# Two-layer hybrid backbone: the low parts of the weights by a negation on ScalarE and an accumulating DMA, with weight sub-blocks as halves of k

## The chip, the cores and the metric

The kernel runs on one NeuronCore of a Trainium2 chip. The metric is the device time of one launch in microseconds (us). Its engines are named as in the profile: PE (TensorE, the matmuls; PEld is its weight load), ACT (ScalarE), DVE (VectorE), POOL (GpSimd), and SP (SyncE, which here only issues DMAs). Each works through its own list of instructions in order.

## What is computed

One sample of 512 latent tokens (a grid of 64 columns) with a context of 256 tokens, 1024 features, goes through two layers. The first mixes by neighbourhood attention (8 heads of 64) beside four bidirectional gated recurrent heads (HGRN2), the second by a short gated convolution; each is followed by a gated feed-forward network (FFN) with 2816 inner features. Shift, scale and gate vectors come from the conditioning vector. All inputs are float32.

```python
def short_conv_mixer(h, w_in, conv_w, conv_b, w_out):
    gate_b, gate_c, u = jnp.split(h @ w_in, 3, axis=-1)
    return (gate_b * dwconv3(gate_c * u, conv_w, conv_b)) @ w_out

def conv_ffn(h, w_up, conv_w, conv_b, w_down):
    a, val = jnp.split(h @ w_up, 2, axis=-1)
    return (jax.nn.gelu(dwconv3(a, conv_w, conv_b), approximate=False) * val) @ w_down
...
for layer in range(DEPTH):
    mod = silu_c @ ada_w[layer] + ada_b[layer]
    shift_m, scale_m, gate_m, shift_f, scale_f, gate_f = jnp.split(mod, 6, axis=-1)
    ...
    h = modulate(rms_norm(x, norm_mix_w[layer]), shift_m, scale_m)
    if is_even:
        y, y_ctx = even_mixer(h, h_ctx, ev_w_in[j], ev_w_out[j], ...)
    else:
        y = short_conv_mixer(h, od_w_in[j], od_conv_w[j], od_conv_b[j], od_w_out[j])
    x = x + gate_m[:, None, :] * y
    h = modulate(rms_norm(x, norm_ffn_w[layer]), shift_f, scale_f)
    x = x + gate_f[:, None, :] * conv_ffn(h, ffn_w_up[layer], ...)
return rms_norm(x, final_norm_w)
```

## The kernel before

**Matmuls in two parts.** Every large product is done in float32r with operands split exactly into a high and a low part. `mm3` (L245) issues three matmuls for one tile of 128 rows of the contraction: high weight by high activation, high weight by low activation, low weight by high activation (L246, L247, L248). The third is the only one that reads the low part of the weights. Activations are feature-major, tiles of 128 features by 512 tokens.

**The weight stream.** All large weights are read once, in the order of a list called `plan` (L157 and on). An entry of the plan is a chunk of 256 columns by up to 1024 rows (1 MB), which SP loads into one of two raw buffers `wraw` of 128 x 2048 (`_load`, L59). A chunk has two sub-blocks. For the dense layers (`cols` L158, `rows_cols` L164) these are halves of the columns: all eight tiles of k, 128 columns each, so that a sub-block is all the weight of one output tile. For the recurrent and attention heads (`two`) the chunk is put together from two column groups. The first two chunks and the last projection (`wide`) have sub-blocks of four k tiles by 256 columns.

**The split.** `Weights.conv` (L65) makes a sub-block's parts: ACT copies the raw weights into `whi` (L84), which rounds them to float32r, and DVE subtracts the copy from the raw weights into `wlo` (L85). `whi` and `wlo` have three buffers each, 128 x 1024. `get(ahead)` (L93) returns the next sub-block and emits the splits up to `ahead` sub-blocks further, so in the dense layers a split stands in the program one sub-block ahead of its use, and its copy waits until PE has read the sub-block three places earlier. A raw buffer is free for the next load when both its sub-blocks are split. Sub-blocks are numbered 0 to 201 in the order of their use below.

**The order of the program.** After a start (norms, first adaptive vectors) come the values of the recurrent heads (sub-blocks 0 to 3, PSUM tiles `pvl`, `pvc`), then the mixer: a list of background tasks (`Weave`) puts the recurrent heads' scans (DVE, with small products `kb`, `qb`, `qi` on POOL), the attention and the adaptive vectors of the later stages (`Ada`, loads `ar` of 256 KB on SP's queue, L443) between the projections' matmuls. The first two output tiles of the output projection (`w_first`, L910, PSUM `pbo00` and `pbo01`) are built up as the attention heads finish, in the order of k = 4, 0, 5, 1, 2, then 6, 7, then 3. From there on the dense rest: `project_back` (L986) multiplies back to 1024 features, two tiles at a time, adds to the stream and collects the norm; its last two tiles go by halves of the tokens (256 each) so that the norm overlaps, with some spare buffers for sub-blocks split ahead (L1001). `quad` (L1054) does the first four tiles of the next stage by halves of the tokens, `pair` (L1046) two tiles of the following ones. `ffn_up` (L1087) takes pairs alternately from the two halves of the up projection (PSUM `ppa`, `ppv`), with the convolution (`conv3`: one ACTIVATE on ACT, L1072, two instructions on DVE), a GELU on ACT and the product. Accumulators have six PSUM buffers in the dense rest. The last projection (`down`, L1194) is token-major.

Of the kernel before, what the change touches and what calls it, by code (L numbers as in the profile page):

```python
# [9 lines left out]
F32 = mybir.dt.float32  # L10
# [28 lines left out]
class Weights:  # L39
    """Streams weight chunks and splits each sub-block exactly into two float32r parts."""  # L40
# [24 lines left out]
    def conv(self):  # L65
        """Split the next sub-block."""
# [18 lines left out]
        self.pin(self.nc.vector.tensor_tensor(lv, rv, hv.bitcast(F32), ALU.subtract))  # L85
# [48 lines left out]
def backbone(ctx: ExitStack, tc: tile.TileContext, a, out, dump=None):  # L134
# [13 lines left out]
    # ---------------------------------------------------------------- pools  # L148
# [6 lines left out]
    # ---------------------------------------------------------------- weight plan  # L155
    ktiled = lambda w: w.rearrange("(k p) c -> p k c", p=P)

    def cols(w, c0):  # L158
        return [([ktiled(w)[:, :, c0 : c0 + 256]], [(0, 0, w.shape[0] // P, j, j + P) for j in (0, P)])]
# [4 lines left out]
    def rows_cols(w, k0, k1, c0):  # L164
        return ([ktiled(w)[:, k0:k1, c0 : c0 + 256]], [(0, 0, k1 - k0, j, j + P) for j in (0, P)])
# [13 lines left out]
    plan += cols(w_in, 3840)  # L179
# [21 lines left out]
    # ---------------------------------------------------------------- constants  # L201
# [18 lines left out]
    # ================================================================ start  # L220
# [13 lines left out]
    def gate(h, src):  # L234
        """Output gate of a recurrent head with its norm weight."""
# [14 lines left out]
    def rms(srcs, n, nm, pool, aux):  # L250
        """Reciprocal root mean square over the features."""
# [35 lines left out]
    with ExitStack() as st:  # L287
# [37 lines left out]
        # (1 + bias) * norm weight  # L325
# [3 lines left out]
        # adaptive shift and scale of latents and context, one feature tile at a time;  # L329
        # row blocks of the weights go to the four column groups of the array  # L330
# [31 lines left out]
        # sum of squares: odd tiles straight on the tensor engine  # L362
# [40 lines left out]
        # lower bounds of the forget gates  # L403
# [27 lines left out]
    # ---------------------------------------------------------------- remaining adaptive vectors  # L431
# [554 lines left out]
    def project_back(nm, src, groups, gate, norm, start=0):  # L986
# [5 lines left out]
        for n, (mp_, gi) in enumerate(steps):  # L992
# [5 lines left out]
            if n == len(steps) - 1:  # L998
                break
# [282 lines left out]
```

## Time and profile before

| | |
|---|---|
| median of 3 runs | 1355.35 us (1355.1 to 1356.38) |
| span of the profiled execution, first to last instruction | 1353.2 us; its device time is not given apart from the runs |
| instructions | 19127 |
| DMA | 172.21 MB, mean 127 GB/s |
| weights: loads of `wraw` | 8 to 44 of each matrix, most of 1024 KB |
| adaptive weights: loads of `ar` | 160 of 256 KB |

The page gives the busy time of each engine and its share of the span, then groups of instructions by source line: the busy time, the mean of one in ns, and how long the engine stood idle ahead of them and for what. A busy PE is not PE at its peak; idle time of an engine that is not the limit costs nothing. In the timeline a row is the start, the length, the engine, the line and the operation with its tiles, and, in brackets, the idle time ahead of it and what ended it.

### The profile page before, as it was taken

How to read it: one execution, taken by the hardware profiler on the slowest of the kernel's cores; microseconds unless marked ns; L12 is line 12 of the kernel's file. 1: busy time of each engine (PE TensorE's matmuls, PEld its weight loads, DVE VectorE, ACT ScalarE, POOL GpSimd, SP SyncE). 2: the span in 40 equal slices, each digit the busy share in tenths (PEclk: the TensorE clock that was granted, in tenths of full speed). 3: DMA queues.
4: the chain of work that ended last, by engine and by line, in shares of the span. 5: the costliest groups of instructions: out<-in, count | busy, mean ns of one | idle time of the engine just before them, and what ended most of it. 6: DMA issues, size and time to landing. Idle time of an engine off the chain costs nothing. (4 is left out here: it accounts for less than half of the span.)

```text
span 1353.2 us, 19127 instructions
## 1 busy us (share of the span) xinstructions
PE 1330.6 (98%) x7736; PEld 1134.4 (84%) x7736; DVE 819.5 (61%) x1354; ACT 527.8 (39%) x815; POOL 84.4 (6%) x87
## 2 busy tenths in 40 slices
PE   7999999999999999999999999999999999999997
PEld 4797888888879888888888898888998888889997
DVE  4668788687777645555566675557766544442333
ACT  4533444555555433333322253223443333333223
POOL 2204322321000000000000000000000000000000
PEclk9999999999999999999999999999999999999999
DMA  9942112466454233333366633444423222332231
GB/s 295 267 127 65 32 32 78 117 159 178 146 168 143 90 117 128 124 118 117 109 192 196 211 126 125 149 143 152 147 86 124 94 94 95 102 101 84 86 110 63
DMA packets 170824, 172.21 MB, mean 127 GB/s; under 512 B 14320, under 2 KB 144752, under 8 KB 170736
## 3 DMA queue, kind: packets, MB, share of 16 engines
q1 hardware_dynamic: 168736, 166.15, 39.3%
q10 hardware_dynamic: 2000, 4.85, 1.4%
q8 instruction: 60, 0.98, 0.3%
q14 instruction: 28, 0.23, 0.1%
HBM read 165.21 MB, written 2.10 MB: 124 GB/s over the span
## 5 line engine op out<-in xcount | busy, mean ns | idle before, releaser
L84 ACT CAST whi<-wraw 128x1024 fp32r<-128x1024 f32 (+1 forms) x202 | 207.8, 1031 | 471.1 <-PE ppv L247 93.5
L85 DVE TENSOR_TENSOR wlo<-wraw,whi 128x1024 fp32r<-128x1024 f32 (+1 forms) x202 | 242.7, 1203 | 218.9 <-ACT whi L84 217.6
L247 PE MATMUL ppa<-hf,whi 128*128 128x512 f32 (+1 forms) x448 | 161.6, 361 | 0.0
L246 PE MATMUL ppa<-hf,whi 128*128 128x512 f32 (+1 forms) x448 | 161.2, 360 | 0.0
L248 PE MATMUL ppa<-hf,wlo 128*128 128x512 f32 (+1 forms) x448 | 160.2, 358 | 0.0
L247 PE MATMUL ppv<-hf,whi 128*128 128x512 f32 x320 | 126.1, 394 | 0.0
L246 PE MATMUL ppv<-hf,whi 128*128 128x512 f32 x320 | 125.8, 393 | 0.0
L248 PE MATMUL ppv<-hf,wlo 128*128 128x512 f32 x320 | 124.3, 388 | 0.0
L462 DVE SCALAR_TENSOR_TENSOR aa<-ar,sil,aa 128x512 f32<-128x512 f32 x140 | 105.1, 751 | 15.2 <-DMA ar<-in_ada_w_dram 13.7
L1198 PE MATMUL pd<-whi,g 128*128 128x256 f32 x352 | 98.1, 279 | 0.0
L1200 PE MATMUL pd<-wlo,g 128*128 128x256 f32 x352 | 98.0, 278 | 0.0
L1199 PE MATMUL pd<-whi,g 128*128 128x256 f32 x352 | 97.7, 278 | 0.0
L246 PEld LDWEIGHTS ppa<-hf,whi 128*128 128x128 f32 x448 | 84.1, 188 | 13.9
L248 PEld LDWEIGHTS ppa<-hf,wlo 128*128 128x128 f32 x448 | 84.1, 188 | 13.2
L247 PEld LDWEIGHTS ppa<-hf,whi 128*128 128x128 f32 x448 | 84.2, 188 | 12.2
L1109 DVE TENSOR_TENSOR ppv<-ppv,cv 128x512 f32<-128x512 f32 x40 | 28.0, 699 | 86.1 <-PE ppv L248 86.1
L246 PE MATMUL pbd<-g,whi 128*128 128x512 f32 (+1 forms) x192 | 72.3, 377 | 0.0
L247 PE MATMUL pbd<-g,whi 128*128 128x512 f32 (+1 forms) x192 | 72.0, 375 | 0.0
L248 PE MATMUL pbd<-g,wlo 128*128 128x512 f32 (+1 forms) x192 | 71.7, 373 | 0.0
L246 PEld LDWEIGHTS ppv<-hf,whi 128*128 128x128 f32 x320 | 60.1, 188 | 13.8
L248 PEld LDWEIGHTS ppv<-hf,wlo 128*128 128x128 f32 x320 | 60.1, 188 | 13.4
L247 PEld LDWEIGHTS ppv<-hf,whi 128*128 128x128 f32 x320 | 60.2, 188 | 11.9
(340 smaller groups left out, 2885.3 us busy)
## 6 DMA issues: line engine op xcount, KB each, us to landing
wraw<-in_ffn_w_up_dram SPq DMA_DIRECT2D x44, 1024.0 KB, 5.0
ar<-in_ada_w_dram SPq DMA_DIRECT2D x160, 256.0 KB, 2.8
wraw<-in_ffn_w_down_dram SPq DMA_DIRECT2D x16, 1024.0 KB, 5.1
wraw<-in_od_w_in_dram SPq DMA_DIRECT2D x12, 1024.0 KB, 5.2
wraw<-in_ev_w_in_dram SPq DMA_DIRECT2D x20, 512.0 KB, 5.3
araw<-in_ada_w_dram SPq DMA_DIRECT2D x16, 512.0 KB, 6.1
wraw<-in_ffn_w_down_dram SPq DMA_DIRECT2D x8, 768.0 KB, 4.9
wraw<-in_ev_w_out_dram SPq DMA_DIRECT2D x4, 1024.0 KB, 6.8
```

What stands on the lines that cost most here:

```text
L84: self.nc.scalar.copy(hv, rv)
L85: self.pin(self.nc.vector.tensor_tensor(lv, rv, hv.bitcast(F32), ALU.subtract))
L246: TE.matmul(o, wh, mh, start=start, stop=False, skip_group_check=True)
L247: TE.matmul(o, wh, ml, start=False, stop=False, skip_group_check=True)
L248: TE.matmul(o, wl, mh, start=False, stop=stop, skip_group_check=True)
L462: pin(V.scalar_tensor_tensor(self.acc[:], raw[:], sil[:, r, 0:1], self.acc[:], ALU.mult, ALU.add))
L1109: V.tensor_tensor(ov[i][:], ov[i][:], t[i][:], ALU.mult)
L1198: TE.matmul(o[i][:, 0:256], gh[:, ts], w[0][:, k - k0], start=k == 0, stop=False)
L1199: TE.matmul(o[i][:, 0:256], gl[:, ts], w[0][:, k - k0], start=False, stop=False)
L1200: TE.matmul(o[i][:, 0:256], gh[:, ts], w[1][:, k - k0], start=False, stop=k == FT - 1)
```

## The change

Three things change.

1. **The low part.** ACT writes the negated weights, rounded to float32r into `wlo` (`scalar.mul` by -1.0, L85 of the changed kernel), and an accumulating DMA on POOL's queue adds the raw float32 weights onto it (L86), which leaves raw minus high, as before. DVE has no part in it. There are 202 such DMAs, most of 512 KB from SBUF to SBUF, 128 rows of 4 KB.
2. **The sub-blocks.** In `cols` and `rows_cols` a sub-block is now half of the k tiles with all 256 columns, so that its rows are contiguous in the raw buffer. The function `blk` picks a tile's weights for one k from the list of sub-blocks.
3. **The order of use.** `pair` fetches the first half of k, does both output tiles with it, then the second half; `project_back` does the same, and its splits ahead (`ws.ahead(4)`, with the spare buffers) come after the first half. `w_first` and `quad` keep their order of k and tiles and take the weights by `blk`. The last chunk of the input projection (L179) becomes two column groups.

Comments are gone in the changed file and lines have moved by two to sixteen.

```diff
     def conv(self):
...
         self.nc.scalar.copy(hv, rv)
-        self.pin(self.nc.vector.tensor_tensor(lv, rv, hv.bitcast(F32), ALU.subtract))
+        self.nc.scalar.mul(lv, rv, -1.0)
+        self.nc.gpsimd.dma_start(lv.bitcast(F32), rv, accum_op=ALU.add)
...
     def cols(w, c0):
-        return [([ktiled(w)[:, :, c0 : c0 + 256]], [(0, 0, w.shape[0] // P, j, j + P) for j in (0, P)])]
+        return [rows_cols(w, 0, w.shape[0] // P, c0)]
...
     def rows_cols(w, k0, k1, c0):
-        return ([ktiled(w)[:, k0:k1, c0 : c0 + 256]], [(0, 0, k1 - k0, j, j + P) for j in (0, P)])
+        h = (k1 - k0 + 1) // 2
+        return ([ktiled(w)[:, k0:k1, c0 : c0 + 256]], [(0, 0, h, 0, 256), (0, h, k1 - k0, 0, 256)])
...
-    plan += cols(w_in, 3840)
+    plan.append(two(w_in, 3840, 3968))
...
+    def blk(w, i, k):
+        n = w[0][0].shape[1]
+        return [v[:, k % n, i * P : (i + 1) * P] for v in w[k // n]]
...
-                mm3(o_first[i][:], w_first[i][0][:, k], w_first[i][1][:, k], hh, hl, k == 4, k == 3)
+                wh, wl = blk(w_first, i, k)
+                mm3(o_first[i][:], wh, wl, hh, hl, k == 4, k == 3)
...
     def project_back(nm, src, groups, gate, norm, start=0):
...
-            w = [ws.get(), ws.get()]
+            w = [ws.get()]
             first, lastg = gi == 0, gi == len(groups) - 1
             if n == len(steps) - 1:
+                w.append(ws.get())
                 break
+            if n < len(steps) - 2 or len(groups) > 1:
+                units(4)
+            mid = k0 + (k1 - k0 + 1) // 2
+            for i in range(2):
+                mms(o, w, i, src, k0, k0, mid, slice(0, T), first, False)
+            w.append(ws.get())
             if n == len(steps) - 2:
                 ws.spare = [(gq, f"q{2 * i}", f"q{2 * i + 1}") for i in range(3)]
                 ws.ahead(4)
-            if n < len(steps) - 2 or len(groups) > 1:
-                units(4)
             for i in range(2):
-                mms(o[i], w[i], src, k0, k0, k1, slice(0, T), first, lastg)
+                mms(o, w, i, src, k0, mid, k1, slice(0, T), False, lastg)
...
     def pair(nm, src):
-        w = [ws.get(), ws.get()]
         o = [acc_t(f"pp{nm}{i}") for i in range(2)]
-        for i in range(2):
-            mms(o[i], w[i], src, 0, 0, KT, slice(0, T), True, True)
+        w = []
+        for k in (0, 4):
+            w.append(ws.get())
+            for i in range(2):
+                mms(o, w, i, src, 0, k, k + 4, slice(0, T), k == 0, k == 4)
         return o
```

**At the start, on ACT.** The rows from the last tile of the first norm on, before: `whi0` and `whi1` are the high parts of sub-blocks 0 and 1, `sqac` is the context's norm (its logarithm reads PE's sum `prc`), `sgq` are gates, `hc` the context's norm tiles.

```order
L270 ACTIVATE h0_7_92<-xs7_117,mod_77,amul_81 128x512
L84 CAST whi0_581<-wraw0_577 128x1024
L264 ACTIVATE sqac_521<-prc_556,epsc_73 128x256
L84 CAST whi1_595<-wraw0_577 128x1024
L265 ACTIVATE sqac_521<-sqac_521 128x256
L418 ACT_TABLE_LOAD
L418 ACTIVATE sgq0_615<-pq0_201 128x512
L270 ACTIVATE hc0_93<-ct0_199,mod_77,amul_81 128x256 x3
```

The same place of the change, where `wlo0` and `wlo1` written by L85 are the negations:

```order
L272 ACTIVATE h0_7_92<-xs7_117,mod_77,amul_81 128x512
L84 CAST whi0_581<-wraw0_577 128x1024
L266 ACTIVATE sqac_521<-prc_556,epsc_73 128x256
L85 ACTIVATE wlo0_582<-wraw0_577 128x1024
L267 ACTIVATE sqac_521<-sqac_521 128x256
L84 CAST whi1_596<-wraw0_577 128x1024
L272 ACTIVATE hc0_93<-ct0_199,mod_77,amul_81 128x256 x2
L85 ACTIVATE wlo1_597<-wraw0_577 128x1024
```

The negation of sub-block 0 stands where the copy of sub-block 1 stood, behind the logarithm, and that copy has moved behind the exponential.

**At the first output columns, on ACT and PE.** ACT of the change from the copy of sub-block 27 on; `gg` is a sigmoid gate, `vn`, `pe`, `pT` and `mnh` are attention's values, exponentials, transposed exponentials and outputs.

```order
L84 CAST whi27_3932<-wraw13_3582 128x1024
L239 ACT_TABLE_LOAD
L239 ACTIVATE gg2_3788<-pg2_3722 128x512
L805 COPY vn3_3764<-pvt3_3765 128x512
L810 COPY vn3_3764<-pvu3_3774 128x256
L830 ACT_TABLE_LOAD
L830 ACTIVATE pe300_3818,sm300_3815<-ps300_3810,sm300_3815 128x512
L244 CAST mgh2_3803<-gg2_3788 128x512
L830 ACTIVATE pe301_3836,sm301_3833<-ps301_3828,sm301_3833 128x512
L855 CAST mnh2_3851<-pno2_3341 128x4x8x16
L840 COPY pT300_3860<-pt300_3855 128x512
L85 ACTIVATE wlo27_3933<-wraw13_3582 128x1024
```

The copy's place and the rows behind it are those of before; the negation is the last row, behind all of them. PE's first matmuls of these columns, before:

```order
L246 MATMUL pbo00_3914<-mgh0_2687,whi26_3766 128x512
L247 MATMUL pbo00_3914<-mgl0_2688,whi26_3766 128x512
L248 MATMUL pbo00_3914<-mgh0_2687,wlo26_3767 128x512
L246 MATMUL pbo00_3914<-mnh0_2974,whi26_3766 128x512
L247 MATMUL pbo00_3914<-mnl0_2975,whi26_3766 128x512
```

The change:

```order
L248 MATMUL pbo00_3944<-mgh0_2705,whi27_3932 128x512
L249 MATMUL pbo00_3944<-mgl0_2706,whi27_3932 128x512
L248 MATMUL pbo01_3945<-mgh0_2705,whi27_3932 128x512
L250 MATMUL pbo00_3944<-mgh0_2705,wlo27_3933 128x512
L248 MATMUL pbo00_3944<-mnh0_2995,whi26_3793 128x512
```

The first matmuls used to read sub-block 26 (all k of the first tile); now they read 27 (k from 4 on, both tiles). PE's last matmuls of the same columns, before:

```order
L246 MATMUL pbo00_3914<-mnh3_4076,whi26_3766 128x512
L247 MATMUL pbo00_3914<-mnl3_4077,whi26_3766 128x512
L248 MATMUL pbo00_3914<-mnh3_4076,wlo26_3767 128x512
L246 MATMUL pbo01_3915<-mnh3_4076,whi27_3904 128x512
L247 MATMUL pbo01_3915<-mnl3_4077,whi27_3904 128x512
L248 MATMUL pbo01_3915<-mnh3_4076,wlo27_3905 128x512
```

The change:

```order
L248 MATMUL pbo00_3944<-mnh3_4106,whi26_3793 128x512
L249 MATMUL pbo00_3944<-mnl3_4107,whi26_3793 128x512
L250 MATMUL pbo00_3944<-mnh3_4106,wlo26_3794 128x512
L248 MATMUL pbo01_3945<-mnh3_4106,whi26_3793 128x512
L249 MATMUL pbo01_3945<-mnl3_4107,whi26_3793 128x512
L250 MATMUL pbo01_3945<-mnh3_4106,wlo26_3794 128x512
```

Sub-block 26 is now read up to the very last row, three matmuls longer; sub-block 29 takes its buffer.

**In the mixer, on POOL.** The change's rows around the first recurrent head's products, where `fg`, `fc` and `tb` are small fills and `wlo7` and `wlo8` the low parts of sub-blocks 7 and 8:

```order
L86 DMA wlo6_1101<-wraw3_914 128x1024
L573 MEMSET fg01_1238 128x2
L86 DMA wlo7_1217<-wraw3_914 128x1024
L560 MEMSET fc01_1232 128x2
L591 MEMSET tb10_1430 128x2
L610 TENSOR_TENSOR kb00_1196<-kn00_1124,cv00_1153 128x256
L610 TENSOR_TENSOR qb00_1198<-qn00_1123,cv00_1153 128x256
L604 TENSOR_TENSOR qi00_1200<-qn00_1123,cv00_1153 128x512
L573 MEMSET fg10_1359 128x2
L86 DMA wlo8_1338<-wraw4_1097 128x1024
```

Before, the same list held the fills and the products alone.

More of the change, by code (lines that the diff above doesn't have):

```diff
@@ L930, in backbone, with mms @@
     HALF = (slice(0, TC), slice(TC, T))
-    def mms(o, w, src, base, k0, k1, c, first, last):
-        wh, wl = w
+    def mms(o, w, i, src, base, k0, k1, c, first, last):
         for k in range(k0, k1):
             hh, hl = src[k]
-            mm3(o[:, c], wh[:, k - base], wl[:, k - base], hh[:, c], hl[:, c], first and k == base, last and k == k1 - 1)
+            wh, wl = blk(w, i, k - base)
+            mm3(o[i][:, c], wh, wl, hh[:, c], hl[:, c], first and k == base, last and k == k1 - 1)
     class Norm:
@@ L1013, in project_back @@
         ws.ahead(4)
-        mms(o[0], w[0], src, k0, k0, k1, A, first, True)
+        mms(o, w, 0, src, k0, k0, k1, A, first, True)
         norm.back(o[0], 6, A, gate)
@@ L1061, in quad @@
                     hh, hl = src[k]
-                    mm3(o[i][:, c], w[i][0][:, k], w[i][1][:, k], hh[:, c], hl[:, c], k == 0 and c.start == 0,
+                    wh, wl = blk(w[i // 2 * 2 : i // 2 * 2 + 2], i % 2, k)
+                    mm3(o[i][:, c], wh, wl, hh[:, c], hl[:, c], k == 0 and c.start == 0,
                         k == KT - 1)
```

8 lines of the change are left out of this document (4 added, 4 removed).

## The prediction, made before the changed kernel was run

> **What bounds the kernel now.** I read the page first, then PE's waits, then short stretches of the timeline around the weight splits.
>
> ```profile
> span 1353.2 us, 19127 instructions
> PE 1330.6 (98%) x7736; PEld 1134.4 (84%) x7736; DVE 819.5 (61%) x1354; ACT 527.8 (39%) x815; POOL 84.4 (6%) x87
> PEclk9999999999999999999999999999999999999999
> L84 ACT CAST whi<-wraw 128x1024 fp32r<-128x1024 f32 (+1 forms) x202 | 207.8, 1031 | 471.1 <-PE ppv L247 93.5
> L85 DVE TENSOR_TENSOR wlo<-wraw,whi 128x1024 fp32r<-128x1024 f32 (+1 forms) x202 | 242.7, 1203 | 218.9 <-ACT whi L84 217.6
> ```
>
> TensorE is busy for 1330.6 of 1353.2 us, with its granted clock in the top tenth in every slice. 22.6 us are not busy, so no edit that leaves the matmuls as they are can win more than that. The 202 copies at 1031 ns on ACT and 202 subtractions at 1203 ns on DVE take 450 us of two engines that have room. What counts is whether a low part is there when its first matmul is due.
>
> ```profile
> PE pkc L584 <- DVE sc L567: 2.1, 2, 1.5
> PE pt L836 <- DVE pe L830: 1.3, 4, 0.5
> 102.00:136.00 34.00, 31.87 (x208) 27.15 (x206) 30.95 (x45) 11.39 (x21) 14.61 (x13) 1.00 0.21 60
> 476.00:510.00 34.00, 34.00 (x150) 27.92 (x149) 16.92 (x20) 12.49 (x17) 0.00 (x0) 1.00 0.33 109
> ```
>
> The first two rows are PE's longest waits for DVE (total, times, longest), 3.4 us together; the others give the busy time of PE, PEld, DVE, ACT and POOL in a stretch, then clock, DMA share and GB/s. In the mixer (102 to 136) DVE is busy for 30.95 of 34 us and PE lacks 2.1. In an FFN (476 to 510) PE has no gap: 34.00 us for 150 matmuls, 0.227 each, so one sub-block of 24 takes 5.4 us.
>
> **How late a low part may be.** One sub-block of the FFN, from its copy to its first low matmul:
>
> ```profile
> 502.52 1.05 ACT L84 CAST whi<-wraw 128x1024 fp32r<-128x1024 f32 x1 [3.95 <-PE ppa L247]
> 503.47 0.77 ACT L1072 ACTIVATE cv<-ppa,vec 128x512 f32<-128x512 f32 x1
> 503.60 1.23 DVE L85 TENSOR_TENSOR wlo<-wraw,whi 128x1024 fp32r<-128x1024 f32 x1 [3.01 <-ACT whi L84]
> 513.99 0.39 PE L248 MATMUL ppv<-hf,wlo 128*128 128x512 f32 x1
> ```
>
> The copy starts when PE gives a buffer of the ring of three back, at 502.52; the low part is read first at 513.99, 11.5 us later, and is ready at 504.83. In the new form ACT takes 1.05 for the copy and as much for the negation, which moves the same elements (by the 0.77 of a 512-element ACTIVATE it could be 1.5). The accumulating transfer, from POOL's issue to its landing, may then take 11.5 - 2.1 = 9.4 us before PE notices, or 8.6 where such an ACTIVATE stands ahead of the negation. I call its length L.
>
> **What L is.** The trace has no accumulating transfer and none from POOL's queue. The nearest rows:
>
> ```profile
> wraw<-in_ffn_w_up_dram SPq DMA_DIRECT2D x44, 1024.0 KB, 5.0
> ar<-in_ada_w_dram SPq DMA_DIRECT2D x160, 256.0 KB, 2.8
> QS<-QS ACTq DMA_DIRECT2D x8, 256.0 KB, 2.9
> KS<-kl ACTq DMA_DIRECT2D x8, 192.0 KB, 3.9
> q1 hardware_dynamic: 168736, 166.15, 39.3%
> ```
>
> A line through 256 KB in 2.8 and 1024 KB in 5.0 gives 3.5 us for 512 KB. An accumulation must also read what it adds to; as 1 MB of traffic it takes 5.0. For POOL's own issue, which no row shows, I allow 1.0. **I take L = 6.0**, nearest to the 1 MB row. The ends are 3.3 (2.9 and an issue of 0.4, the adding free) and 11.5 (two passes of 5.0 one after the other, issue 1.5).
>
> The Trainium skill, in "Collectives: The Full Stack", section "The bandwidth ceiling: the fold count and why AG ≠ RS ≠ AR", says that an adding transfer runs at half of a copy's rate because it reads two sources, not because adding costs. With the fixed 2.0 us and 436 GB/s of "DMA: Bandwidth & Descriptors", section "Anatomy of one DMA", that makes an estimate of 4.4 us; the same fit gives 4.4 for the 1 MB load that took 5.0 here, so this trace is slower than the page, and by the page the sum would be about +3 us.
>
> **Where L = 6 shows.** The steady stages hide it with 2.6 us or more. The short places, in order:
>
> ```profile
> 59.34 1.03 ACT L84 CAST whi<-wraw 128x1024 fp32r<-128x1024 f32 x1
> 61.16 0.47 ACT L264 ACTIVATE sqac<-prc,epsc 128x256 f32<-128x256 f32 x1 [0.79 <-PE prc L263]
> 61.53 1.04 ACT L84 CAST whi<-wraw 128x1024 fp32r<-128x1024 f32 x1
> 65.41 0.28 PE L537 MATMUL pvl<-wlo,h 128*128 128x256 f32 x1
> ```
>
> *Start, sub-block 0.* The new order puts ACT's logarithm (L264 here), which waits for PE, between copy and negation. The negation takes the slot of the second copy: 61.53 + 1.04 = 62.57, + 6.0 = 68.6, against 65.41: **+3.2 us**. PE runs its queue in order and can put nothing in its place.
>
> ```profile
> 370.50 0.59 ACT L838 COPY pT<-pt 128x512 f32<-128x512 f32 x1
> 375.64 0.40 PE L248 MATMUL pbo<-mgh,wlo 128*128 128x512 f32 x1
> ```
>
> *First output columns, sub-block 27.* The order of ACT shows its negation behind the whole group of sigmoid, exponentials and copies, after the first pT copy, which ends at 371.1; 372.1 + 6.0 = 378.1. As the half with k from 4 to 7 it is now wanted first, one matmul after the place at 375.64: 375.9. **+2.3 us** (the ACT and PE rows under the change).
>
> ```profile
> 395.45 0.39 PE L248 MATMUL pbo<-mnh,wlo 128*128 128x512 f32 x1
> 395.65 2.00 ACT L84 CAST whi<-wraw 128x1024 fp32r<-128x1024 f32 x2 [1.69 <-PE pbo L247]
> 396.13 0.39 PE L248 MATMUL pbo<-mnh,wlo 128*128 128x512 f32 x1
> 402.31 0.39 PE L248 MATMUL pbo<-mnh,wlo 128*128 128x512 f32 x1
> 395.00:405.00 10.00, 10.00 (x45) 8.24 (x44) 7.63 (x9) 4.22 (x5) 0.00 (x0) 1.00 1.03 342
> 398.07 0.38 SPq L59 DMA_DIRECT2D wraw<-in_ev_w_out_dram  x1
> ```
>
> *Output projection, sub-block 29* takes 26's buffer. 26 now serves both tiles of the first columns, so its last matmuls are those at 396.13 and no longer those at 395.45 (the PE rows under the change): its copy moves by 0.68 from 395.65 to 396.33. Copy and negation end at 398.4, + 6.0 = 404.4, against 402.31: +2.1. It falls in ten microseconds whose DMA share is 1.03 already; I add 1.5, less than half of a 1 MB load. **+3.6.**
>
> ```profile
> 406.28 1.05 ACT L84 CAST whi<-wraw 128x1024 fp32r<-128x1024 f32 x1 [3.40 <-DMA wraw<-in_ev_w_out_dram]
> 409.95 0.63 ACT L958 ACTIVATE sqf<-xT 128x512 f32<-128x512 f32 x1 [2.62 <-DVE xT L953]
> 413.13 0.38 SPq L59 DMA_DIRECT2D wraw<-in_ffn_w_up_dram  x1
> 418.56 0.28 PE L248 MATMUL pbo<-mnh,wlo 128*128 128x256 f32 x1
> 431.11 0.28 PE L248 MATMUL ppa<-hf,wlo 128*128 128x256 f32 x1
> ```
>
> *Sub-blocks 32 and 36.* A raw buffer is now given back by the transfer. The load for 32 and 33, issued at 398.07 when 29's subtraction ended, is issued at 405.9 (404.4 + 1.5) and takes 5.0 to 8.2 (398.07 to 406.28); with 6 it lands at 411.9. Two copies, a square of 0.63 and two negations make 416.7, + 6.0 = 422.7, against 418.56 + 3.6: **+0.5**. The load for 36, at 413.13 now, follows at 422.7 and lands 5.0 later; copy, square, negation (2.7) and 6.0 make 436.4, against 431.11 + 4.1: **+1.2**.
>
> ```profile
> 673.28 1.05 ACT L84 CAST whi<-wraw 128x1024 fp32r<-128x1024 f32 x1 [3.95 <-PE ppv L247]
> 682.41 0.40 PE L248 MATMUL pbd<-g,wlo 128*128 128x512 f32 x1
> 680.00:782.00 102.00, 102.00 (x450) 83.41 (x449) 63.53 (x98) 25.18 (x28) 0.00 (x0) 1.00 0.65 204
> ```
>
> *First FFN's projection back.* Its shortest sub-blocks have 682.41 - 673.28 = 9.1 us, so L may be 7.0; they come at four places, and loads hold 0.65 of the DMA engines: a quarter of a microsecond each, **+1.0**.
>
> **What else moves.** ACT gains 202 x 1.03 = 208 us and stands at 736 of 1353, DVE loses 243; neither is near its end. In the dense stages a load follows the second split of its buffer and is wanted three copies later, 3 x 5.5 - 2.3 = 14.2 us; less 5.0 for the load and 5.8 because the buffer comes back later (1.05 + 6.0 against 1.23), 3.4 are left: hidden. On POOL the transfers stand in order among the mixer's products (the POOL rows under the change); both wait for an ACT that is busy 11.39 of 34 us, and the low parts there have time, as this mixer sub-block's copy and first low matmul show, 27.4 us apart:
>
> ```profile
> 153.09 1.03 ACT L84 CAST whi<-wraw 128x1024 fp32r<-128x1024 f32 x1
> 180.52 0.39 PE L248 MATMUL pf<-h,wlo 128*128 128x512 f32 x1
> ```
>
> In the pairs of the dense stages both tiles now end within 2.7 us instead of 5.4; six accumulators cover that. DVE's relief returns part of the 3.4 us: **-1.0** (between 0 and -3.4).
>
> **Sum:** 3.2 + 2.3 + 3.6 + 0.5 + 1.2 + 1.0 - 1.0 = +10.8 us. The median of the runs lies 2.2 us above this execution's span, and I move both alike: 1355.35 + 10.8 = **1366.2 us**.
>
> **Rivals.**
> *All covered.* With L at 4.2 or less the start costs at most 1.4, sub-blocks 27 and 29 0.5 and 0.3, with up to 1.5 more for the crowd there; less 1.0 that is at most +2.7: 1355 to 1358. For it: the 2.9 of the SBUF-to-SBUF row. Against: 192 KB took 3.9 on the same queue.
> *DVE's relief wins, faster.* In the mixer the subtraction stands in DVE's order behind a copy that waits for PE (217.6 us of DVE's idle time ended with such a copy), and the scans that feed PE stand behind it. Without it up to 3.4 us return; at L = 3.3 the stalls add to under 1: 1355.35 - 3.4 + 0.6 = 1352.6 or less. It decides if L is under 3.8 and these waits hang on the subtraction; but a scan that is long itself stays.
> *Transfers collide, L = 7 to 9.* q1's 39.3% for 166.15 MB is 3.2 us of all engines per MB. The 102 us of the projection back hold 450 matmuls, 19 sub-blocks, 10 MB: a share of 0.65 + 0.31, or 1.27 if an accumulation counts double, and over 1.0 it stretches. L = 8 adds 2 to sub-blocks 0, 27, 29 and 36 and 1.5 to the four places: 1380. L = 9 adds 3 to the one, 2.5 to the others and 0.4 to each of 40 FFN pairs: 1404. The Trainium skill knows a second route there, in "SBUF — State Buffer", section "Who interferes with whom": while DVE runs certain copies, the descriptors of a transfer issued by GpSimd wait. No row here shows it.
> *The adding itself is slow.* At L = 11.5 a buffer's turn is 2.1 + 11.5 + 5.4 = 19.0, a third of which is 6.3 per sub-block instead of 5.5; 160 dense sub-blocks make +130 us, 1485. It decides from 9.4 on.
>
> **Chances.** Forecast (L 5 to 7) 0.48; all covered 0.18; relief 0.09; collisions 0.17; slow adding 0.08. 0.2% is 2.7 us, about what a measurement of this kernel can tell from no change. Faster 0.09, same 0.18, slower 0.73. The forecast's own range is 1361 (L = 5) to 1371 (L = 7). The range from 1353 to 1400 leaves out the slow adding, most of the relief and the end of the collisions, 0.17.
>
> **What would show it.** The rows of the accumulating transfers give L: 5 to 7 right, under 4.2 or over 9 wrong. PE's waits for wlo should be 3 us at the first pvl, 2 at the first pbo of sub-block 27, 3 to 4 near 402, and none in the FFN pairs; if the pairs show waits, the sum is wrong by a multiple. If the waits at L584 are gone, the relief was sized too low. DVE should fall to about 577 us and ACT rise to 736.

## The result and the profile after

| | before | after |
|---|---|---|
| median, us | 1355.37 (4 runs, 1355.1 to 1356.38) | 1460.38 (4 runs, 1448.28 to 1462.9) |
| ratio | | 1.0755, 95% interval 1.0714 to 1.0795 |
| span of the profiled execution, us | 1353.2 | 1461.1 |

The changed kernel is 105 us slower, ten times the forecast's +10.8 and outside its range. The page of the changed kernel, the busy rows, TensorE's clock, the DMA engines' busy tenths and POOL's queue (packets, MB, share of the engines' time):

```profile
span 1461.1 us, 19760 instructions
PE 1368.3 (94%) x7736; PEld 1156.8 (79%) x7736; DVE 609.3 (42%) x1152; ACT 714.0 (49%) x1017; POOL 242.9 (17%) x289
PEclk9999999899999999999999989999999999999999
DMA  9885225777678489878899995998958888786774
q0 software_dynamic: 29088, 103.82, 38.6%
```

DVE lost its 202 subtractions and ACT gained 202 negations, as the change says. PE has the same 7736 matmuls, but stands idle for 1461.1 - 1368.3 = 92.8 us instead of 22.6 (+70.2), and its busy time has grown by 37.7; together that is the 107.9 us of the span. The DMA row is at 7 to 9 tenths through most of the kernel. Before, an FFN's stretch from 476 to 510 us had 0.33; what is new is POOL's queue q0.

PE's waits in the changed kernel (total us, times, longest), longest first, those that are new:

```profile
PE pbo L248 <- DVE xT L961: 12.4, 2, 7.5
PE pbd L250 <- DMA wlo<-wraw: 12.2, 6, 3.7
PE pbo L250 <- DMA wlo<-wraw: 11.1, 5, 3.6
PE pnm L973 <- DVE sqam L969: 6.9, 1, 6.9
PE ppa L250 <- DMA wlo<-wraw: 5.9, 3, 2.8
PE pt L838 <- DVE pe L832: 5.6, 5, 2.7
PE ppv L250 <- DMA wlo<-wraw: 4.8, 4, 2.1
PE pd L1216 <- DMA wlo<-wraw: 4.7, 4, 2.5
PE pt L838 <- DVE sm L831: 4.0, 1, 4.0
PE pvl L539 <- DMA wlo<-wraw: 3.3, 2, 2.1
```

They fall into three kinds. The low part is late (`wlo`): 12.2 + 11.1 + 5.9 + 4.8 + 4.7 + 3.3 = 42.0 us in 24 waits, in every stage. PE waits behind the norm of a projection back (`xT`, `sqam`): 19.3 us in three. PE waits in the attention (`pt`): 9.6 us, where it was 1.3. The sum, less that 1.3, is 69.6 of the 70.2.

The longer busy time is for the most part TensorE's granted clock. Its mean over the span is 0.998 before and 0.974 after: in the changed kernel it stands at 0.50 in 14 stretches of 3.4, 6.8 or 10.2 us, 68 us in all, each at a wait of PE (the last section shows one), besides one at the start and one at the end that the kernel before has too. Below they are called half clock. Matched one by one in their order with the matmuls of e1_kdve (below, the same 7736, in another order at 306 places), those that start at 0.50 take 28 us longer, waits left aside, and all others 9 us. The next three rows show it too: 0.58, 0.80 and 0.79 us for matmuls that took 0.28, 0.39 and 0.39 before.

```profile
67.99 0.58 PE L539 MATMUL pvl<-wlo,h 128*128 128x256 f32 x1 [2.07 <-DMA wlo<-wraw]
396.03 0.80 PE L250 MATMUL pbo<-mgh,wlo 128*128 128x512 f32 x1 [2.35 <-DMA wlo<-wraw]
427.80 0.79 PE L250 MATMUL pbo<-mgh,wlo 128*128 128x512 f32 x1 [3.62 <-DMA wlo<-wraw]
```

These are the prediction's first three places, sub-blocks 0, 27 and 29: 2.1, 2.4 and 3.6 us against 3.2, 2.3 and 3.6. So the places that were worked out came near to what was worked out; the loss is elsewhere. The DMA issues (KB each, median us from issue to landing) and the longest waits for loads:

```profile
wlo<-wraw POOLq DMA_DIRECT2D x190, 512.0 KB, 6.1
wraw<-in_ffn_w_up_dram SPq DMA_DIRECT2D x44, 1024.0 KB, 6.5
ar<-in_ada_w_dram SPq DMA_DIRECT2D x160, 256.0 KB, 5.7
...
SPq L59 <- DMA wlo<-wraw: 923.4, 90, 32.5
ACT whi L84 <- DMA wraw<-in_ffn_w_up_dram: 68.8, 19, 11.6
ACT whi L84 <- DMA wraw<-in_ffn_w_down_dram: 38.1, 6, 11.2
```

The transfer's median, 6.1, is the prediction's L = 6.0. But the loads have grown with it: `wraw` from 5.0 to 6.5, `ar` from 2.8 to 5.7. Where SP's queue stands with a load of a raw buffer, a transfer's landing now ends the wait (the row L59, 90 times; before, DVE's subtraction did, as often). ACT's copies, which used to wait for PE to give a buffer back, wait for loads: 106.9 us in the last two rows alone, where the longest such row before was this one.

```profile
ACT whi L84 <- DMA wraw<-in_od_w_in_dram: 5.8, 2, 3.5
```

One pair of the first FFN shows how that comes to PE; the rows are from the timeline of the changed kernel (start, length, engine, and in brackets the idle time and what ended it), first POOL, then ACT, then PE:

```profile
612.53 0.87 POOL L86 DMA_DIRECT2D wlo<-wraw  x1 [2.12 <-ACT wlo L85]
...
622.59 1.05 ACT L84 CAST whi<-wraw 128x1024 fp32r<-128x1024 f32 x1 [5.67 <-DMA wraw<-in_ffn_w_up_dram]
...
622.97 0.51 PE L250 MATMUL ppv<-hf,wlo 128*128 128x512 f32 x1 [1.14 <-DMA wlo<-wraw]
631.54 0.79 PE L250 MATMUL ppa<-hf,wlo 128*128 128x512 f32 x1 [2.77 <-DMA wlo<-wraw]
```

The transfer issued at 612.53 takes 10.4 us, and the load beside it, issued at 610.57 when another transfer of 8.9 us had landed, takes 12.0. The transfer ends PE's wait at 622.97; the load ends ACT's at 622.59, and the copy that it released is followed by a negation and a transfer for which PE waits again, up to 631.54. The second kind of wait, at the end of the mixer's projection back, on ACT and then DVE and PE:

```profile
457.38 1.04 ACT L84 CAST whi<-wraw 128x1024 fp32r<-128x1024 f32 x1 [11.65 <-DMA wraw<-in_ffn_w_up_dram]
458.33 0.62 ACT L966 ACTIVATE sqf<-xT 128x512 f32<-128x512 f32 x1
...
458.99 0.69 DVE L969 TENSOR_TENSOR sqaf<-sqaf,sqf 128x512 f32<-128x512 f32 x1 [11.59 <-ACT sqf L966]
459.60 0.48 DVE L961 SCALAR_TENSOR_TENSOR xT<-pbo,mod,xT 128x256 f32<-128x256 f32 x1
...
460.13 0.58 PE L248 MATMUL pbo<-mnh,whi 128*128 128x256 f32 x1 [7.47 <-DVE xT L961]
```

A copy for the next stage, split ahead, waits 11.65 us for its load. The square of the norm stands behind it on ACT, the sum of squares behind that on DVE, and behind that the addition that frees PE's accumulator: 7.5 us, in which no low part is missing.

### The profile page after: what moved, and what is told of

The parts are those of the page before. It is cut to its first block, busy times and chain, and to the rows that moved or that the text cites. A ratio compares the mean times of both kernels' runs of the same rounds, so it can differ in the third digit from the quotient of the medians.

```text
span 1461.1 us, 19760 instructions
## 1 busy us (share of the span) xinstructions
PE 1368.3 (94%) x7736; PEld 1156.8 (79%) x7736; DVE 609.3 (42%) x1152; ACT 714.0 (49%) x1017; POOL 242.9 (17%) x289
## 3 DMA queue, kind: packets, MB, share of 16 engines
q0 software_dynamic: 29088, 103.82, 38.6%
## 5 line engine op out<-in xcount | busy, mean ns | idle before, releaser
L86 POOL DMA_DIRECT2D wlo<-wraw x202 | 174.3, 863 | 1081.8 <-ACT wlo L85 992.6
L85 ACT ACTIVATE wlo<-wraw 128x1024 fp32r<-128x1024 f32 (+1 forms) x202 | 209.4, 1037 | 0.0
L1089 DVE SCALAR_TENSOR_TENSOR cv<-ppa,vec,cv 128x511 f32<-128x511 f32 x44 | 32.8, 750 | 134.9 <-ACT cv L1088 134.9
L250 PE MATMUL pbd<-g,wlo 128*128 128x512 f32 (+1 forms) x192 | 75.5, 393 | 12.2 <-DMA wlo<-wraw 12.2
L248 PE MATMUL pbd<-g,whi 128*128 128x512 f32 (+1 forms) x192 | 75.8, 395 | 0.0
L249 PE MATMUL pbd<-g,whi 128*128 128x512 f32 (+1 forms) x192 | 75.0, 390 | 0.0
```

What stands on the lines that cost most here:

```text
L85: self.nc.scalar.mul(lv, rv, -1.0)
L86: self.nc.gpsimd.dma_start(lv.bitcast(F32), rv, accum_op=ALU.add)
L248: TE.matmul(o, wh, mh, start=start, stop=False, skip_group_check=True)
L249: TE.matmul(o, wh, ml, start=False, stop=False, skip_group_check=True)
L250: TE.matmul(o, wl, mh, start=False, stop=stop, skip_group_check=True)
L1089: V.scalar_tensor_tensor(t[:, 1:], src[:, : T - 1], w0, t[:, 1:], ALU.mult, ALU.add)
```

## The experiments

What was to be told apart, with the letters of the expectations: that the transfers land late and hold the raw buffers, so that ACT's list blocks behind a copy (A); that the transfer's own length makes the low part late (B); that transfers and loads share the DMA engines (C); that the new order of the sub-blocks costs by itself (D); and, without a letter, that DVE and POOL hinder each other. All ratios are to the kernel before, run beside on the same chip; it took 1355.4 to 1356.1 us on each, so that the runs can be set beside each other too.

| run | what it is | median, us | ratio (95%) |
|---|---|---|---|
| e1_kdve | new order, DVE subtracts | 1357.49 | 1.0009 (1.0000 to 1.0019) |
| e2_copy | plain transfer, no adding | 1387.36 | 1.0240 (1.0207 to 1.0273) |
| e3_raw4h | four raw buffers of half a chunk | 1404.24 | 1.0357 (1.0342 to 1.0373) |
| e4_noar | 157 of 160 loads `ar` left out | 1412.03 | 1.0418 (1.0398 to 1.0439) |
| e5_traffic | e1 and transfers beside | 1819.11 | 1.3416 (1.3397 to 1.3436) |
| e6_sqdve | squares on DVE | 1472.09 | 1.0847 (1.0828 to 1.0865) |
| e7_mixer | transfers for sub-blocks 4 to 25 alone | 1369.28 | 1.0088 (1.0063 to 1.0113) |
| e8_raw4h_sqdve | e3 and e6 | 1396.93 | 1.0299 (1.0286 to 1.0312) |
| e9_mixer_bmdve | e7, `bm` on DVE | 1359.52 | 1.0022 (1.0012 to 1.0031) |
| e10_raw4h_copy | e3 and e2 | 1375.40 | 1.0146 (1.0131 to 1.0162) |
| e11_traffic | e1 and transfers beside, mended | 1382.73 | 1.0198 (1.0184 to 1.0212) |
| e12_raw4h_noar | e3 and e4 | 1390.77 | 1.0249 (1.0231 to 1.0267) |

**e1_kdve: the order alone.** The changed kernel with before's subtraction.

```diff
-        self.nc.scalar.mul(lv, rv, -1.0)
-        self.nc.gpsimd.dma_start(lv.bitcast(F32), rv, accum_op=ALU.add)
+        self.pin(self.nc.vector.tensor_tensor(lv, rv, hv.bitcast(F32), ALU.subtract))
```

> The changed kernel with DVE's subtraction back in place of the negation and the transfer; the k halves and their order of use stay. Theory A (the raw buffers: a buffer comes back only when a transfer has landed, the next load starts later, and ACT, which runs in order, stands behind a copy that waits for that load): 1353 to 1358 us, no wait of PE for a low part. Theory B (the transfer's own length makes each low part late): the same. Theory C (transfers and loads share the DMA engines): the same. Theory D (the order of use by k halves costs): 1400 or more.

1357.49 us: the halves of k cost about 1 us, so D is out. All else comes from the way of the low part.

**e2_copy: no adding.** The transfer copies the raw weights over the negation, so the low parts are the whole raw weights.

```diff
-        self.nc.gpsimd.dma_start(lv.bitcast(F32), rv, accum_op=ALU.add)
+        self.nc.gpsimd.dma_start(lv.bitcast(F32), rv)
```

> The accumulating transfer becomes a plain copy of the same 512 KB from POOL's queue, so the low part holds the raw weights and the adding is left out; negation, order and waits stay. If reading the destination is what makes transfers long (C), the transfer takes 3.5 us alone instead of 4.5 and the loss of 105 us falls to 50 or less, 1400. If the loss comes from when a raw buffer returns and not from the traffic (A), the transfer is at most 1 us shorter and about a third of the loss goes, 1425. Theory B: 1 us less at each late part, 1440.

1387.36 us, 73 less. POOL's queue and its DMA issues in this kernel:

```profile
q0 software_dynamic: 28320, 103.82, 19.1%
wlo<-wraw POOLq DMA_DIRECT2D x190, 512.0 KB, 3.9
```

The same 103.82 MB take half the share of the engines, the transfer's median falls from 6.1 to 3.9, and that of the up projection's loads to 5.2. So 70% of the loss goes with the adding, as in C's case (50 us or less left). What stays, 30 us over e1, has transfers that PE waits for at few places (`pbo` 4.4 us), the attention's 9 us and 7 us of waits behind squares.

**e3_raw4h: the raw buffers.** Half a chunk per buffer, four buffers, one load of 512 KB per sub-block: a load now waits for one transfer instead of two, and SBUF holds as much as before.

```diff
-        raw = self.pool.tile([P, 2048], F32, tag="wraw", name=f"wraw{self.nload}", bufs=2)
+        raw = self.pool.tile([P, 1024], F32, tag="wraw", name=f"wraw{self.nload}", bufs=4)
...
-        while self.nload <= min(c + 1, len(self.plan) - 1):
+        while self.nload < len(self.subs) and self.subs[self.nload][0] <= c + 1:
```

> Raw buffers of half a chunk, four instead of two whole ones in the same space: each sub-block is loaded by itself (512 KB) and its buffer returns when its own transfer has landed. Theory A: loads start up to 5.5 us earlier, ACT's waits for weight loads (150 us now) fall under 40, the long waits of PE for the residual and norm sums (7.6, 7.0 and 5.0 us) go, 1375 to 1395 us. Theory B: the transfer is as long as before, 1440 or more. Theory C: traffic is the same, 1440 or more.

1404.24 us, 56 less, 9 above A's case and far under those of B and C, with the transfers hardly shorter (5.8 us at the median, 10.2 at the longest). ACT's waits for weight loads fall from 153 to 53 us. PE's waits for low parts and behind the norm:

```profile
PE pbo L248 <- DMA wlo<-wraw: 11.0, 5, 3.2
PE pbd L248 <- DMA wlo<-wraw: 7.3, 3, 3.3
PE pbo L246 <- DVE xT L961: 6.4, 2, 4.7
...
PE pnm L973 <- DVE sqam L969: 3.5, 1, 3.5
```

The waits in the pairs (`ppa`, `ppv`) are gone, and of those in the last projection (`pd`) 0.4 us is left. They came from the raw buffers' late return, not from the transfer's own length.

**e4_noar: fewer loads beside.** The adaptive weights from the fourth piece on are not loaded; the old piece is used again, so this kernel leaves out most of the adaptive vectors' values.

```diff
+            if n >= 3:
+                self.raw[n] = self.raw[n - 3]
+                return
-            raw = ap_.tile([P, T], F32, tag="araw", name=f"ar{n}", bufs=3)
+            raw = ap_.tile([P, T], F32, tag=f"araw{n}", name=f"ar{n}", bufs=1)
```

> The later adaptive weights are loaded for three blocks only and these are used again, so 157 loads of 256 KB (40 MB of 166) are left out and with them most of the adaptive vectors' values; DVE's work on them stays. Theory C (sharing of the DMA engines): with a quarter of the loads gone the median transfer falls from 6.1 to about 5 and half of the loss goes, 1405. Theory A: only as far as the weight loads get shorter, 1425 to 1440. Theory B: 1440 or more.

1412.03 us, 48 less, nearer to C's case (1405) than to A's (1425 or more). The transfer's median is 5.6 and that of the loads of the up projection 5.7. Loads that have nothing to do with the change take part in the loss, by lying beside it.

**e5_traffic: a miss.** Transfers whose result nobody reads, beside e1's subtraction.

```diff
+        if self.nsub >= 38:
+            for h in range(n * w // 512):
+                self.nc.gpsimd.dma_start(self.scr, hi[:, h * 512 : h * 512 + 512].bitcast(F32), accum_op=ALU.add)
```

> The first experiment's kernel (k halves, DVE's subtraction), and beside it, from sub-block 38 on, two accumulating transfers of 256 KB for each sub-block from the high part onto an idle constant (84 MB in all) that nobody waits for; the raw buffers return as before the change. Theory C (the DMA engines are shared and traffic alone does it): the loads stretch as in the changed kernel and most of the dense stages' loss comes, 1400 or more. Theory A (traffic hurts only because buffers return late): loads stretch to 6 us, which the raw buffers still cover, 1355 to 1365 us. Theory B (the low part's own lateness): 1355 to 1358.

1819.11 us, and it tells nothing of the question. Both transfers of a sub-block add onto one target, so each waits for the one before, and until then they hold the buffer of `whi`, as ACT's row shows:

```profile
ACT whi L84 <- DMA cst<-whi: 736.1, 121, 14.8
```

**e6_sqdve: what stands behind the look-ahead copy.** The squares of the norm move from ACT to DVE.

```diff
-            S.activation(self.sq[:, c], xT[m][:, c], AF.Square)
+            V.tensor_tensor(self.sq[:, c], xT[m][:, c], xT[m][:, c], ALU.mult)
```

> The changed kernel with the squares for the norm sums (two lines of Norm.back) on DVE instead of ACT, where they stand behind the copies that look ahead. Theory A in its form that ACT stands behind a copy that waits for a load: the three waits of 7.6, 7.0 and 5.0 us of PE for the residual and norm sums shrink to under 2 each, and with them the slow matmuls that follow each, 1430 to 1442 us. If the sums are late for another reason, 1455 to 1462.

1472.09 us, not a gain. PE's waits for `xT` and `sqam` are gone, and others stand in their place:

```profile
PE ppa L248 <- ACT hf L987: 18.2, 2, 12.0
PE ppc L248 <- ACT hm L987: 12.3, 1, 12.3
```

The scaled norm tiles `hf` and `hm` are ACT's too and stand behind copies that wait for loads, `hm` behind one of 9.87 us. The block on ACT is real, but the square was only the first to meet it. The expectation took the victim for the cause.

**e8_raw4h_sqdve: the same with the buffers mended.** e3's and e6's edits together.

> The third experiment's kernel (four raw buffers of half a chunk) with the squares on DVE as well. If both remove separate parts of theory A's chain, 1385 to 1393 us (1404 less the waits of 6.4 and 3.5 and half of the slow matmuls); if the squares are late there for another reason, 1402 to 1406.

1396.93 us, 7 less than e3 and between the two cases. The waits behind squares that e3 had (6.4 + 3.5 us) are gone, and none for `hf` or `hm` takes their place; part of it is lost again, since the waits for low parts grow at `pbd` from 7.3 to 9.9 us and at `pbo` from 11.0 to 12.4.

**e7_mixer: the transfers where DVE is the limit.** Only sub-blocks 4 to 25 use the transfer.

```diff
+        if 4 <= self.nsub < 26:
+            self.nc.scalar.mul(lv, rv, -1.0)
+            self.nc.gpsimd.dma_start(lv.bitcast(F32), rv, accum_op=ALU.add)
+        else:
+            self.pin(self.nc.vector.tensor_tensor(lv, rv, hv.bitcast(F32), ALU.subtract))
```

> Negation and transfer only for sub-blocks 4 to 25, those of the mixer and the attention, where DVE is busiest and low parts have 15 us and more; DVE's subtraction elsewhere, k halves throughout. If DVE's relief there is worth what the waits of PE for DVE amount to (2.1 and 1.3 us), 1352.5 to 1355, faster than before; if those waits are the scans' own, 1355 to 1358; POOL's products standing behind transfers could cost 2 to 4, 1360.

1369.28 us, 12 over e1 and above every case. DVE's relief wins nothing: PE's wait at `pkc` is 2.3 us, as before. And no transfer is late here. What is new are the waits of `pt` (5.9 and 4.1 us), and DVE's and POOL's timelines of this kernel show them:

```profile
272.17 5.40 DVE L248 TENSOR_TENSOR kl<-kT,KS 64x768 fp32r<-64x768 f32 x1
299.29 4.71 DVE L835 TENSOR_SCALAR pe<-pe,sm 128x512 f32<-128x512 f32 x1
...
272.32 4.42 POOL L783 TENSOR_TENSOR bm<-nam,rb 128x256 f32<-128x256 f32 x6
299.31 4.39 POOL L783 TENSOR_TENSOR bm<-nam,rb 128x256 f32<-128x256 f32 x6
```

An exponential's scaling that takes 0.49 us takes 4.71 when POOL's group `bm` starts in the same moment, and `kl` 5.40 where it otherwise takes 0.95. Both end just behind the group, by 0.8 and 0.3 us. In POOL's list `bm` now stands behind transfers that wait for ACT's negations, and so it starts later (272.3 and 299.3 us, in e1 267.2 and 292.9), beside other instructions of DVE than before. The changed kernel has the same, for instance this row beside its `bm` at 306.94:

```profile
306.98 4.71 DVE L832 TENSOR_SCALAR pe<-pe,sm 128x512 f32<-128x512 f32 x1
```

**e9_mixer_bmdve: that group on DVE.**

```diff
-                    G.tensor_tensor(v(b_[:, z]), v(nam[:, z]), rb[:, :, e].rearrange("p r (g j) -> p g r j", g=2),
+                    V.tensor_tensor(v(b_[:, z]), v(nam[:, z]), rb[:, :, e].rearrange("p r (g j) -> p g r j", g=2),
```

> The kernel of e7_mixer (negation and accumulating transfer for sub-blocks 4 to 25 alone, DVE's subtraction for all others) with the six subtractions per head pair that make bm (L780) on DVE instead of POOL. If the stalls of pt behind pe and sm (5.9 and 4.1 us in e7_mixer) come from DVE and POOL working at the same time, they go and the time falls from 1369.3 to 1357-1361; if they come from the order or from the transfers, bm on DVE takes nothing away (24 instructions more on DVE) and the time is 1367 or more.

1359.52 us, as expected: 10 us come back, and six `bm` take 2.1 us on DVE. Those groups start no earlier than in e7 (278.2 and 304.3 us), so it was not their lateness. The collision is the cause of the third kind of wait.

**e10_raw4h_copy: both main edits.**

> Four raw buffers of half a chunk (as e3_raw4h, 1404.2) and a plain copy in place of the accumulation (as e2_copy, 1387.4); the low parts are then the raw weights. If all of the loss comes from transfers that land late, through the raw buffers and through the wait for the low part, each of the two changes takes away most of what the other leaves: 1362-1370. If the traffic of the transfers (19% of the DMA engines here) costs apart from their own landing, 1375-1387. If only the accumulation matters, no change against e2_copy: 1384-1390.

1375.40 us, at the edge of the middle case. The copy takes away 29 of the 47 us over e1 that e3 leaves, the buffers 12 of the 30 that e2 leaves; 18 remain. They stand at `pbo` (3.9 us for low parts and 3.3 for `xT`, all up to 435 us), one place of 3.0 in the projection back of the first FFN, and 5 us lost at half clock. These are waits again, and the run shows no clear cost of the traffic apart from them.

**e11_traffic: traffic alone, mended.** One transfer per target and sub-block, from sub-block 38 on three quarters of the change's bytes there.

```diff
+        if self.nsub >= 38:
+            self.nc.gpsimd.dma_start(self.scr, hi[:, 0:512].bitcast(F32), accum_op=ALU.add)
+            if n * w >= 768:
+                self.nc.gpsimd.dma_start(self.scr2, hi[:, 512:768].bitcast(F32), accum_op=ALU.add)
```

> DVE's subtraction as in e1_kdve (1357.5), and beside it, from sub-block 38 on, one accumulating transfer of 256 KB and one of 128 KB per sub-block from whi onto two constants that are read no more: three quarters of the change's added bytes, on separate targets, and no instruction waits for their landing but the next use of a whi buffer. If the loss comes only from what waits for the transfers (raw buffers, low parts), 1357-1362; if the traffic by itself makes the loads of raw weights late enough that ACT and then PE wait, 1370-1400.

1382.73 us, 25 over e1, in the second case. Two rows of its DMA issues and waits:

```profile
wraw<-in_ffn_w_up_dram SPq DMA_DIRECT2D x44, 1024.0 KB, 6.5
ACT whi L84 <- DMA hgm<-whi: 70.1, 15, 8.1
```

The loads take 6.5 us as in the changed kernel, yet the FFNs' up projections have no wait of PE over 0.4 us: a slower load by itself is hidden, as the prediction said. 21 of the 25 us fall between 748 and 816, in the projection back of the first FFN, where the DMA engines' share is 0.93 (0.47 in e1). There the transfers take so long that they hold `whi` back (second row), and PE's longest wait, 7.0 us, is again one for `xT`, so that traffic and waiting are not apart in this run either.

**e12_raw4h_noar: buffers and quiet.** e3's and e4's edits together, all transfers kept.

> Four raw buffers of half a chunk (as e3_raw4h, 1404.2) and 157 of the 160 loads ar left out (as e4_noar, 1412.0); the accumulating transfers stay, all 202. The loads ar that are left out make the numbers of the adaptive vectors other than the reference's. If the loss comes from late raw buffers, and the competing loads made them late, what is left are the waits for the low part that had no cover in the prediction (sub-blocks 0, 27, 29, some 1.3 + 2.2 + 3.4 + 2.4 us in e3_raw4h), a rest of the waits behind the squares (0 to 6 us) and the clock after them (2 to 5 us): 1366-1380. If the accumulating transfers cost by themselves, whatever loads beside them and with buffers enough: 1390-1402.

1390.77 us, above the first case and at the foot of the second. Its reason, a cost of the transfers by themselves, is not needed, though, if by that more than late low parts is meant: PE's waits and the clock account for the time.

```profile
PE pbo L248 <- DMA wlo<-wraw: 13.1, 5, 4.1
...
PE pt L841 <- DVE pe L835: 6.8, 6, 2.6
```

With 1.1 us at sub-block 0, 2.3 at one place of the first FFN's projection back, 3 behind squares and 8 us lost at half clock, these rows make some 34 us; the kernel is 33 over e1, which has 3 us of the same kinds. Not counted in the expectation were two waits of 2.7 us in the second layer's projection back, and the attention's collisions, which the order put in this kernel and not in e3.

## Why the prediction was wrong

**What held, in part by luck.** L is 6.1 at the median, 6.0 was taken; but that was a 1 MB row's 5.0 from the trace before and 1.0 for the issue, and a transfer with nothing beside it takes 4.6. The rest of the 6.1 is stretch, which the sum had at few places. Sub-blocks 0, 27 and 29 are 2.1, 2.4 and 3.6 us late (3.2, 2.3, 3.6); their transfers took 4.7, 6.0 and 8.8 us, and the third came out because 1.5 had been added there for the crowd. The loss was put on the side of slower, with 0.73, and DVE's relief is worth nothing (e7), not the 1.0 that was subtracted. DVE's busy time fell to 609.3 and ACT's rose to 714.0 us (577 and 736). The Trainium skill ("Collectives: The Full Stack", section "The bandwidth ceiling: the fold count and why AG ≠ RS ≠ AR") says of the adding step of a ring collective that it runs at half of a copy's rate, for its two source reads. The engines' time agrees here, 38.6% against 19.1%. The prediction's estimate of 4.4 us from the skill's figures is near what the 18 transfers took that lay beside no other transfer and no load of a raw buffer, 4.6 at the median, where plain ones took 2.9 (e2). The other 184 took 6.55 at the median and up to 11.0.

**The step that failed** is "14.2 us; less 5.0 for the load and 5.8 because the buffer comes back later ..., 3.4 are left: hidden". It took the load's 5.0 from a trace in which the DMA engines' share was 0.33 there, and one L for all. With the medians of after, 6.5 and 6.1, 1.8 us would still be left. But transfer and load stand in the same chain *and* share the DMA engines, so that they are long together: 12.0 and 10.4 at 612, where the rest goes below zero. The chain can be followed from sub-block 29 on: its transfer lands at 427.76, the next load into that buffer runs to 436.93, the transfers of 32 and 33 to 446.91, the next load to 457.28, and the copy of 36 starts at 457.38. The prediction's own sign for this step, waits in the FFN pairs, came with 10.7 us in seven waits. e3 gives the chain slack and the pairs' waits go (-56 us); e2 makes the transfers short (-73 us); e4 takes loads away that lie beside (-48 us). These are not three costs to add: each breaks the same chain, and e2 and e3 together (e10) win 85, not 129.

**What followed from it and had no term.** A late load stops ACT in front of the copy, and with it all that stands behind on ACT: the squares, and without them `hf` and `hm` (e6). The prediction moved the copies of sub-blocks 32 and 36 (+0.5 and +1.2) and counted the square's own 0.63 us, but not who waits for the square. At the copy of sub-block 36 PE waited 7.5 us, and three such waits make 19.3. Most of the longer waits go with a stretch of half clock, about 28 us in all, also without a term.

**The first FFN's projection back** was priced at +1.0, a quarter of a microsecond at each of four places. It lost 12.2 us to `pbd`, 6.9 to `sqam` and 8 to the clock. The rival of colliding transfers had the cause: its share of 1.27 for these 102 us (0.65 + 2 x 0.31) counts the adding double, which is what the engines show, and the measured share from 723 to 868 is 0.95. It was priced only as a longer L at the places already listed and 0.4 at each FFN pair, and so ended at 1404.

**Not thought of:** `bm` on POOL. The order showed the transfers among POOL's rows, and the prediction asked only when the transfers would come, not what comes later behind them. It costs 10 us in e7, and 8 in the changed kernel by PE's rows.

**Open.** How the loss in the projection back of the first FFN divides between slower transfers and held buffers. e11 was to say and holds `whi` there. The other runs say a part: from the first matmul of `pbd` to the first of `ppc` it takes 123.5 us in e1, 152.5 in the changed kernel, 141.6 with more buffers (e3), 130.5 without the adding (e2), 130.1 without the `ar` loads (e4) and 128.6 with both more buffers and no `ar` (e12). So in this stage less traffic takes away 22 of the 29 us and more buffers 11, while in the pairs each of these edits removes every wait of a microsecond or more. Not run were the negation without any transfer, so that the price of ACT's 209 us by themselves is not shown, and the transfers with the old order of the sub-blocks. None of the versions beats the kernel before; the nearest, e1 and e9, have nothing that would pay for the change.

## What to carry to other kernels

- When a step moves from an engine to a DMA, its buffers come back at the landing. Write the whole turn of the ring (load, split, transfer, load) with the durations that the transfers have *beside each other*, tails and not medians, and widen the ring before anything else.
- An in-order engine that looks ahead for the next stage puts every wait for a load in front of the work of this one. Ask of each look-ahead copy what stands behind it, and what behind that.
- Work put into a quiet queue delays what was there. Look at what the old instructions will now run beside.

## What the runs showed of the hardware

**TensorE's clock is halved at waits.** PE in the changed kernel, around the wait of 6.9 us (the rows between are alike):

```profile
861.74 0.28 PE L250 MATMUL pbd<-g,wlo 128*128 128x256 f32 x1
868.88 1.19 PE L973 MATMUL pnm<-sqam,ones 128*128 128x256 f32 x2 [6.86 <-DVE sqam L969]
...
873.28 0.41 PE L249 MATMUL pbd<-g,whi 128*128 128x256 f32 x1
873.50 0.32 PE L250 MATMUL pbd<-g,wlo 128*128 128x256 f32 x1
873.66 0.28 PE L248 MATMUL pbd<-g,whi 128*128 128x256 f32 x1
```

The starts lie 0.21 us apart up to 873.3 and 0.12 from 873.66 on. The two stretches in a view of windows (busy time of PE, PEld, DVE, ACT and POOL, then granted clock, DMA share, GB/s):

```profile
868.90:873.30 4.40, 4.40 (x19) 4.22 (x20) 1.91 (x5) 2.28 (x6) 0.00 (x0) 0.50 1.06 170
873.60:878.00 4.40, 4.40 (x39) 4.40 (x39) 2.65 (x7) 0.01 (x1) 0.00 (x0) 1.00 1.07 361
```

The clock is 0.50 and then 1.00, and the second stretch holds 39 matmuls where the first holds 19. The stretches at 0.50 last 3.4, 6.8 or 10.2 us. Of the 16 waits of PE of 1.9 us and more from sub-block 0 on, 14 have one, the shortest of them 1.91 us; the wait of 2.07 at 67.99 has it from 68.0 to 71.4. Two have none, one of them of 2.69 us (at 311.7). The Trainium skill ("TensorE: Matmul & The Clock Gate", section "HAM oscillation — how this bites in real kernels") speaks of idle gaps over some 3.4 us; here gaps of 1.9 to 2.8 us also did it, and not each time.

**DVE beside POOL.** A single DVE instruction stood for a whole group of six POOL instructions (0.49 to 4.71 us, e7 and the changed kernel alike), though by the trace it had started 0.02 to 0.15 us ahead of the group in e7. In e1, where both engines also work side by side there, `kl` takes 1.41 us at the most. The Trainium skill ("SBUF — State Buffer", section "Who interferes with whom") says that the two share a pair of ports, which, for certain forms of DVE instruction, one of them holds for a whole instruction. That agrees with the stretch; that the one waits for six of the other's in a row is more than the page says.
